# Four instead of two column tiles in the first matmul block, and a last LayerNorm split between VectorE, PSUM and GpSimd, in a decoder layer

## The chip, the cores and the metric

One NeuronCore of a Trainium2 chip runs the whole layer as one launch. The metric is the device time of a run in microseconds. The engines are named as the profile names them: PE is TensorE (PEld its weight loads), DVE is VectorE, ACT is ScalarE, POOL is GpSimd, SP is SyncE, which here only starts transfers.

## The reference

One layer of a hybrid decoder on 512 tokens of width 1024, all in fp32:

```
proj = x @ w_in                          # q, k, v of three token mixers, and gates
m = mixer(...)                           # differential, stick-breaking and dilated attention,
                                         # gated, merged, @ w_out
x = layer_norm(ALPHA * x + m, ln1_g, ln1_b)
c = square(relu(x @ w_up)) @ w_down
ple = sigmoid(x @ w_ple_gate) * (p @ w_ple)
x = layer_norm(ALPHA * x + c + ple, ln2_g, ln2_b)

def layer_norm(x, g, b):
    mu = x.mean(-1); var = square(x - mu).mean(-1)
    return (x - mu) * rsqrt(var + 1e-5) * g + b
```

## The kernel before

Every fp32 operand is split into a rounded high part (`h`, by an ACT cast, line 213) and the remainder (`l`, by a DVE subtraction, line 215), and each product is three matmuls: high by high, high by low, low by high. Weights come in chunks through a ring of SBUF buffers, loaded from SP's queue and split ahead of their use by `pump`. A list `items` holds the matmul groups in their order; the program walks it once and puts between the items the evictions, the splits and the steps of the attention heads. The framework then fixes, for each engine, a static order of instructions and the semaphores between them; an engine works through its own list in order. Dependencies in PSUM are kept for whole tiles (one bank of 512 fp32 columns), not for columns of one.

**The start.** `first_item` (line 293) makes the first two column tiles, T0 (a query tile of the stick-breaking heads) and T1 (a key tile), together: for each of the eight row blocks k of x and w it loads x[k] (256 KB) and w of both tiles (128 KB for one k, 256 KB for a pair of them), splits both, and issues six matmuls of 512 columns. The loads alternate: x0, w0, x1, w1-2, x2, x3, w3-4 and so on. The first `AHEAD` = 4 of them go out at once, the next waits for a matmul of the warm-up on zeros (line 1390). After the block, `t_item` (line 258) makes one further column tile at a time, T2 and T3 first, each from a 512 KB chunk with 24 matmuls (k = 0 to 7); PE then also does the logits of the first head (line 131), which need the split query and key tiles. The low part of the key tile is DVE's line 101 with output `sb_ka`.

**The end.** `plain` (line 1292) makes the last products of the MLP for four row tiles tt = 0 to 3, in halves of 512 columns; for tile three the second half is cut in two groups of 256 columns (`ends`), each in a PSUM bank of its own. Tiles 0 to 2 take their LayerNorm from `layer_norm_act` (line 807): a DVE addition with a row sum, squares on ACT, the power -0.5 on POOL (line 818), centring on DVE (line 820), and a last DVE pass with bias per half, before the store (`rest`, line 822). For tile two that last pass is held back and issued behind the first addition of tile three (`held`, line 1336). Tile three adds its PSUM to the SBUF rows `acc`, takes `bn_stats` per piece (line 1340), and `last_norm` (line 1349) then computes the mean and variance, the inverse root by ACT's square root, a reciprocal and one Newton step on DVE, the centring (line 1359) and the last pass with three stores (lines 1367 and 1369). So that the square root's table is there, line 1981 runs one square root ahead of the last stage.

Of the kernel before, what the change touches and what calls it, by code (L numbers as in the profile page):

```python
# [55 lines left out]
def trunk(tc, a, out):  # L56
    nc = tc.nc
    es = ExitStack()
    with es:
# [73 lines left out]


        RING, RAW = 6, 7
        ORDERED, AHEAD = 17, 4
        loads, chunks, placed = [], [], []
        lows = deque(maxlen=4)
        marks = deque(maxlen=4)
# [153 lines left out]
        def first_item():  # L293

            w = a["w0"].rearrange("p k m -> p (k m)")
            cs = {}
            for k in range(8):
                x_chunk(k)
                if k in (0, 1, 3, 5, 7):
                    n = 256 if k in (0, 7) else 512  # L300
                    c = chunk_of(load(w[:, 256 * k:256 * k + n], n, True))
                    for i in range(n // 256):
                        cs[k + i] = (c, 256 * i)

            def mm(ps):
                for k in range(8):
                    c, o = cs[k]
                    for i, (m, x) in enumerate((("h", xh), ("l", xh), ("h", xl))):
                        for t in range(2):
                            nc.tensor.matmul(ps[t], c[m][:, o + t * P:o + t * P + P], x[k], start=k == 0 and i == 0,  # L310
                                             stop=k == 7 and i == 2, skip_group_check=True)

            def ev(ps):
                for t in range(2):
                    t_evac(*order[t][1:])(ps[t])
            item([cs[k][0] for k in (0, 1, 3, 5, 7)], mm, ev, bank=lambda: (at_bank(), at_bank()))

        HB = slice(0, 256)
        HC = slice(256, 512)
# [484 lines left out]
                                                      ap=[[0, P], [1, 512]]))  # L804
                lnc[n] = t

        def layer_norm_act(ts, sm, g, b, fin):
# [9 lines left out]
            nc.vector.tensor_scalar(r, r, EPS, None, op0=OP.add)  # L817
            nc.gpsimd.tensor_tensor(r, r, mhalf, OP.pow)
            for h in range(2):
                nc.vector.scalar_tensor_tensor(ts[h], ts[h], nmu, lnc[g][h], op0=OP.add, op1=OP.mult)  # L820

            def rest():
                for h in range(2):
                    nc.vector.scalar_tensor_tensor(ts[h], ts[h], r, lnc[b][h], op0=OP.mult, op1=OP.add)
                    fin(h, ts[h])
            return rest

# [463 lines left out]

        def plain(cs, c2, c4, kept):

            sums, held = {}, []
            s6 = slot("bn6e")[:, :18].rearrange("p (a b) -> p a b", b=6)

            ends = [(0, slice(0, 512)), (1, slice(0, 256)), (1, slice(256, 512))]

            def part(tt, half, cc):
                n = cc.stop - cc.start  # L1300
                r = tt % 2
                p, cp = {(0, 0): (2, c2), (1, 0): (4, c4)}.get((tt // 2, half), (0, []))

                def mm(ps):
                    for c, m in zip(cp, (5, 6)):
                        down_mm(ps, m, p, r, c, p == 2 and m == 5, False)
                    for i in range(4):
                        h, lo = left[ND - 1, tt // 2, i % 2]
                        q = slice((i // 2) * 256 + r * P, (i // 2) * 256 + r * P + P)
                        c = cs[i % 2, half]  # L1310
                        s = slice((i // 2) * 512 + cc.start, (i // 2) * 512 + cc.stop)
                        nc.tensor.matmul(ps[:, :n], h[:, q], c["h"][:, s], start=i == 0 and not p, stop=False,
                                         skip_group_check=True)
                        nc.tensor.matmul(ps[:, :n], h[:, q], c["l"][:, s], start=False, stop=False,
                                         skip_group_check=True)
                        nc.tensor.matmul(ps[:, :n], lo[:, q], c["h"][:, s], start=False, stop=i == 3,
                                         skip_group_check=True)

                def ev(ps):
                    t = acc[tt, half]  # L1320
                    if tt < 3:
                        if not half:
                            sums[tt] = small("lsm", 2)
                        nc.vector.scalar_tensor_tensor(t, t, 1.0, ps, op0=OP.mult, op1=OP.add,
                                                       accum_out=sums[tt][:, half:half + 1])
                        if half:
                            def fin(h, y):
                                (nc.sync if h else nc.scalar).dma_start(
                                    out[0, tt * P:tt * P + P, 512 * h:512 * h + 512], y)
                            rest = layer_norm_act([acc[tt, 0], acc[tt, 1]], sums[tt], "ln2_g", "ln2_b", fin)  # L1330
                            if tt == 2:
                                held.append(rest)
                            else:
                                rest()
                        return
                    i = nc.vector.tensor_add(t[:, cc], t[:, cc], ps[:, :n])
# [3 lines left out]
                    nc.vector.bn_stats(s6[:, ends.index((half, cc)), :], t[:, cc])  # L1340
# [5 lines left out]
                item(free, mm, ev, need=list(cs.values()) + list(cp),  # L1346
                     bank=(lambda: kept["y", r]) if p == 4 else at_bank if tt == 3 else None)

            def last_norm():
                ts = [acc[3, 0], acc[3, 1]]  # L1350
                mv = small("mv", 2)
                nc.vector.bn_aggr(mv, s6)

                hv, y, r = [small("lr", 1) for _ in range(3)]
                nc.vector.tensor_scalar(hv, mv[:, 1:2], EPS, -0.5, op0=OP.add, op1=OP.mult)
                nc.scalar.activation(y, hv, AF.Sqrt, scale=-2.0)

                def center(h):
                    nc.vector.scalar_tensor_tensor(ts[h], ts[h], mv[:, 0:1], lnc["ln2_g"][h], op0=OP.subtract,
                                                   op1=OP.mult)  # L1360
                center(0)
                nc.vector.reciprocal(y, y)
                nc.vector.scalar_tensor_tensor(r, y, hv, y, op0=OP.mult, op1=OP.mult)
                nc.vector.scalar_tensor_tensor(r, r, 1.5, y, op0=OP.add, op1=OP.mult)
                center(1)
                for i, (h, cc) in enumerate(ends):
                    nc.vector.scalar_tensor_tensor(ts[h][:, cc], ts[h][:, cc], r, lnc["ln2_b"][h][:, cc],
                                                   op0=OP.mult, op1=OP.add)
                    (nc.scalar if i == 1 else nc.sync).dma_start(
                        out[0, 3 * P:4 * P, 512 * h + cc.start:512 * h + cc.stop], ts[h][:, cc])  # L1370

            for tt in range(3):
                for half in range(2):
# [541 lines left out]
        for n, it in enumerate(items):  # L1915
# [62 lines left out]
                ln_consts("ln1_g", "ln1_b")  # L1978
            if n == ln2_at[0]:

                i = nc.scalar.activation(small("rt", 1), ident[:, 0:1], AF.Sqrt)
                tc.add_manual_dep(getattr(i, "ins", i), lows[-1].name, mybir.DependencyInfo(
                    mybir.DependencyClass.Sync, mybir.DependencyReason.DATA), reason="behind the last gate")
# [54 lines left out]
def _layout(x, p, w_in, da_lambda, da_norm, w_branch_da, w_branch_sb, w_branch_dil, w_out, ln1_g, ln1_b,  # L2038
# [17 lines left out]
    def quarters(w):  # L2056
# [5 lines left out]
        "xn": c(x2.reshape(4, 128, 1024).transpose(1, 0, 2)),  # L2062
        "pT": c(p[0, 0].T.reshape(2, 128, 512).transpose(1, 0, 2)),
        "w0": c(np.stack(tiles[0:2], axis=2).reshape(128, 8, 256)),
        "wt": c(np.stack(tiles[2:])),
        "wv": c(np.stack(vs)),

# [36 lines left out]
```

## Time and profile before

| | us |
|---|---|
| median of three runs (1046.08 to 1046.97) | 1046.86 |
| the profiled execution's own time | 1046.86 |
| its span in the profile | 1044.8 |
| PE busy | 1033.2 |
| DVE busy | 778.0 |
| ACT busy | 588.1 |
| POOL busy | 179.4 |

The span runs from the first to the last record of one execution; the 2.06 us between it and the time lie outside of what the profiler shows. In the views below a row of the timeline is: start, duration, engine, line and operation, output<-inputs, shape, count, and in brackets the engine's idle time ahead of it with what ended it. In a table of windows each engine has its busy time and, in brackets, the number of its instructions.

### The profile page before, as it was taken

The page shows a single profiled execution, that of the slowest core. Times are in us where ns is not written, and L with a number is a line of the kernel's source. Part 1 is how long each engine was busy: PE and PEld are TensorE (multiplying, and loading weights), DVE is VectorE, ACT ScalarE, POOL GpSimd, SP SyncE. Part 2 cuts the span into 40 slices and gives each one's busy share as a digit, 9 for nine tenths or more (in the row PEclk, how much of TensorE's full clock was granted, in tenths as well). Part 3 has the DMA queues.
Part 4 walks back from the last instruction along what each step waited for, and adds up shares of the span by engine and source line. Part 5 has one row for each costly group of instructions (what it writes and reads, how often), then busy time and mean ns, then how long its engine had stood idle before and what let it go on. Part 6 is the DMA issues. An engine that isn't in the chain of part 4 may idle for free.

```text
span 1044.8 us, 15084 instructions
## 1 busy us (share of the span) xinstructions
PE 1033.2 (99%) x5462; PEld 881.3 (84%) x5462; DVE 778.0 (74%) x1392; ACT 588.1 (56%) x1006; POOL 179.4 (17%) x275
## 2 busy tenths in 40 slices
PE   8999999999999999999999999999999999999996
PEld 6887788889888888888888888888999889889885
DVE  6888577768874657789666895798768877877966
ACT  6666445535444545676653753776666556556651
POOL 0013421020212111311211132101221111111000
PEclk9999999999999999999999999999999999999998
DMA  8348999294896996698998998389999999999602
GB/s 321 114 149 269 241 271 267 89 278 141 255 289 170 312 263 157 213 250 278 292 337 275 314 321 261 115 252 302 331 328 345 304 306 281 328 293 338 191 32 81
DMA packets 74346, 260.09 MB, mean 249 GB/s; under 512 B 9144, under 2 KB 10056, under 8 KB 74272
## 3 DMA queue, kind: packets, MB, share of 16 engines
q0 software_dynamic: 33616, 120.40, 44.3%
q1 hardware_dynamic: 40080, 137.81, 36.9%
q8 instruction: 43, 0.70, 0.3%
q10 hardware_dynamic: 576, 0.92, 0.2%
q14 instruction: 31, 0.25, 0.1%
HBM read 256.98 MB, written 111.17 MB: 352 GB/s over the span
## 4 chain that ended last, share of the span: by engine, by line
PE 97%; DVE 1%; DMA 1%; ACT 0%; SPq 0%; issue 0%; DVEq 0%
PE mm L87 11%; PE mm L88 10%; PE mm L89 10%; PE at L1212 4%; PE at L1213 4%; PE at L1214 4%; PE at L558 3%; PE at L560 3%; PE at L559 3%; PE mm L455 2%; PE mm L457 2%; PE mm L456 2%; PE at L89 1%; PE at L87 1%; PE at L88 1%; PE at L849 1%
## 5 line engine op out<-in xcount | busy, mean ns | idle before, releaser
L213 ACT CAST wh<-raw 128x1024 fp32r<-128x1024 f32 x254 | 265.9, 1049 | 241.8 <-PE mm L88 129.1
L215 DVE TENSOR_TENSOR wl<-raw,wh 128x1024 fp32r<-128x1024 f32 x254 | 308.9, 1221 | 119.9 <-ACT wh L213 117.7
L87 PE MATMUL mm<-xhT,wh 128*128 128x512 f32 x304 | 120.8, 397 | 0.0
L89 PE MATMUL mm<-xhT,wl 128*128 128x512 f32 x304 | 119.1, 392 | 0.0
L88 PE MATMUL mm<-xlT,wh 128*128 128x512 f32 x304 | 119.0, 391 | 0.0
L1212 PE MATMUL at<-wh,hh 128*128 128x512 f32 x188 | 73.7, 392 | 0.0
L1213 PE MATMUL at<-wl,hh 128*128 128x512 f32 x188 | 73.7, 392 | 0.0
L87 PE MATMUL mm<-x1hT,wh 128*128 128x256 f32 x256 | 73.6, 288 | 0.0
L1214 PE MATMUL at<-wh,hl 128*128 128x512 f32 x188 | 73.1, 389 | 0.0
L88 PE MATMUL mm<-x1lT,wh 128*128 128x256 f32 x256 | 72.2, 283 | 0.0
L89 PE MATMUL mm<-x1hT,wl 128*128 128x256 f32 x256 | 71.8, 283 | 0.0
L89 PEld LDWEIGHTS mm<-xhT,wl 128*128 128x128 f32 x304 | 57.1, 188 | 12.1
L87 PEld LDWEIGHTS mm<-xhT,wh 128*128 128x128 f32 x304 | 57.2, 188 | 11.6 <-issue 0.4
L88 PEld LDWEIGHTS mm<-xlT,wh 128*128 128x128 f32 x304 | 57.2, 188 | 10.5
L87 PEld LDWEIGHTS mm<-x1hT,wh 128*128 128x128 f32 x256 | 48.8, 190 | 4.6 <-ACT up L1146 2.8
L88 PEld LDWEIGHTS mm<-x1lT,wh 128*128 128x128 f32 x256 | 48.8, 191 | 1.5
L89 PEld LDWEIGHTS mm<-x1hT,wl 128*128 128x128 f32 x256 | 48.6, 191 | 0.0
L1049 POOL DMA_DIRECT2D usum<-in_wu_dram x32 | 27.4, 883 | 86.7 <-DVE wl L215 63.0
L1214 PEld LDWEIGHTS at<-wh,hl 128*128 128x128 f32 x188 | 35.3, 188 | 7.7
L1212 PEld LDWEIGHTS at<-wh,hh 128*128 128x128 f32 x188 | 35.5, 189 | 6.0
L1213 PEld LDWEIGHTS at<-wl,hh 128*128 128x128 f32 x188 | 35.5, 189 | 5.6
L1049 POOL DMA_DIRECT2D dsum<-in_wd_dram x28 | 24.0, 874 | 93.7 <-DVE wl L215 63.0
(606 smaller groups left out, 2673.6 us busy)
## 6 DMA issues: line engine op xcount, KB each, us to landing
usum<-in_wu_dram POOLq DMA_DIRECT2D x48, 512.0 KB, 9.1
dsum<-in_wd_dram POOLq DMA_DIRECT2D x42, 512.0 KB, 9.1
raw<-in_wt_dram SPq DMA_DIRECT2D x38, 512.0 KB, 5.6
msum<-in_wgm_dram POOLq DMA_DIRECT2D x36, 512.0 KB, 9.0
raw<-usum SPq DMA_DIRECT2D x32, 512.0 KB, 7.7
raw<-dsum SPq DMA_DIRECT2D x28, 512.0 KB, 8.1
raw<-in_wd_dram SPq DMA_DIRECT2D x25, 512.0 KB, 5.9
raw<-msum SPq DMA_DIRECT2D x24, 512.0 KB, 7.1
```

Of the source, the lines that this page charges most:

```text
L87: nc.tensor.matmul(ps, wh, xh, start=start, stop=False, skip_group_check=True)
L88: nc.tensor.matmul(ps, wh, xl, start=False, stop=False, skip_group_check=True)
L89: nc.tensor.matmul(ps, wl, xh, start=False, stop=stop, skip_group_check=True)
L213: i = nc.scalar.copy(h, raw)
L215: i = nc.vector.tensor_sub(lo, raw, h.bitcast(F32))
L558: nc.tensor.matmul(ps, h[:, q], c["h"][:, n], start=go, stop=False, skip_group_check=True)
L559: nc.tensor.matmul(ps, h[:, q], c["l"][:, n], start=False, stop=False, skip_group_check=True)
L560: nc.tensor.matmul(ps, lo[:, q], c["h"][:, n], start=False, stop=end, skip_group_check=True)
L1049: i = nc.gpsimd.dma_start(o, i, accum_op=OP.add, max_dma_last_dim=4096)
L1212: nc.tensor.matmul(ps, h[:, q], c["h"][:, s], start=go, stop=False, skip_group_check=True)
L1213: nc.tensor.matmul(ps, h[:, q], c["l"][:, s], start=False, stop=False, skip_group_check=True)
L1214: nc.tensor.matmul(ps, lo[:, q], c["h"][:, s], start=False, stop=end, skip_group_check=True)
```

## The change

Three things are changed together.

1. The first block takes four tiles in its first step. A new input `w1` holds the k = 0 part of the weights of T2 and T3 (128 x 256, 128 KB). It is loaded third, behind x0 and w0, split, and used for six matmuls into the banks of T2 and T3 right behind the first six; `t_item` then starts at k = 1 for these two tiles (21 matmuls instead of 24), though its 512 KB load stays whole. `AHEAD` and the number of ordered loads go up by one.
2. The last passes of tile two leave DVE: ACT multiplies each half by the inverse root, POOL adds the bias, then comes the store.
3. Tile three keeps three of its four quarter pieces in PSUM: the sum is made in place in the bank, `bn_stats` and the centring work there, and the last DVE pass writes to SBUF. The first quarter stays in SBUF, and POOL does its whole last part (centre and scale, gain, bias). The two groups of the second half now lie in one bank. The inverse root is POOL's addition of epsilon and its power -0.5; ACT's square root, the reciprocal, the Newton step and the early square root for the table are gone. There are four stores of 256 columns instead of three.

```diff
-        ORDERED, AHEAD = 17, 4
+        ORDERED, AHEAD = 18, 5
...
+        begun = []
         def t_item(nt, name, j):
...
+            k0 = 1 if nt < 4 else 0
             def mm(ps):
                 c = cs[0]
-                for k in range(8):
+                for k in range(k0, 8):
...
-            item(cs, mm, t_evac(name, j))
+            item(cs, mm, t_evac(name, j), bank=(lambda: begun[nt - 2]) if k0 else None)
...
+                if k == 0:
+                    both = chunk_of(load(a["w1"], 256, True))
+            def step_of(ps, c, o, k):
+                (the six matmuls of one k)
             def mm(ps):
                 for k in range(8):
...
+                    step_of(ps, *cs[k], k)
+                    if k == 0:
+                        begun.extend(mm_bank() for _ in range(2))
+                        step_of(begun, both, 0, 0)
...
             def rest():
                 for h in range(2):
+                    if last:
+                        nc.scalar.activation(ts[h], ts[h], AF.Copy, scale=r)
+                        nc.gpsimd.tensor_tensor(ts[h], ts[h], lnc[b][h], OP.add)
+                    else:
+                        nc.vector.scalar_tensor_tensor(ts[h], ts[h], r, lnc[b][h], op0=OP.mult, op1=OP.add)
                     fin(h, ts[h])
...
-                    i = nc.vector.tensor_add(t[:, cc], t[:, cc], ps[:, :n])
-                    if held:
-                        with tc.issue_after(getattr(i, "ins", i)):
-                            held.pop()()
-                    nc.vector.bn_stats(s6[:, ends.index((half, cc)), :], t[:, cc])
+                    if not half:
+                        nc.vector.tensor_add(t[:, HB], t[:, HB], ps[:, HB])
+                        nc.vector.bn_stats(s6[:, 0, :], t[:, HB])
+                    c = cc if half else HC
+                    nc.vector.tensor_add(ps[:, c], ps[:, c], t[:, c])
+                    nc.vector.bn_stats(s6[:, 1 + ends.index((half, cc)), :], ps[:, c])
...
+                    if half not in held:
+                        held[half] = at_bank()
+                    return held[half]
...
-                (square root on ACT, reciprocal, Newton step, two centrings, three passes, three stores)
+                nc.gpsimd.tensor_scalar(r, mv[:, 1:2], EPS, None, op0=OP.add)
+                nc.gpsimd.tensor_tensor(r, r, mhalf, OP.pow)
...
+                t = ts[0][:, HB]
+                nc.gpsimd.tensor_scalar(t, t, mv[:, 0:1], r, op0=OP.subtract, op1=OP.mult)
+                nc.gpsimd.tensor_tensor(t, t, lnc["ln2_g"][0][:, HB], OP.mult)
+                nc.gpsimd.tensor_tensor(t, t, lnc["ln2_b"][0][:, HB], OP.add)
+                center(1, slice(0, 512))
+                center(0, HC)
+                for i, (h, cc) in enumerate(((1, HB), (1, HC), (0, HC))):
+                    scaled(h, cc)
+                    store(nc.scalar if i == 1 else nc.sync, h, cc)
+                store(nc.scalar, 0, HB)
...
-                i = nc.scalar.activation(small("rt", 1), ident[:, 0:1], AF.Sqrt)
```

In the order of instructions that the framework makes of it, the following differs besides. ACT and DVE evict T0 and T1 one right behind the other, where a weight split stood between them before. The logits of the first head stand behind 17 matmuls of T2; before they stood behind all 24 of T2 and three of T3. The first matmul of tile three's last group waits for a count of DVE's that is reached with the statistics of the group before. On ACT's queue the store of the POOL quarter stands ahead of the store of columns 768 to 1023. Some evictions in the last MLP stage change places by a few instructions.

More of the change, by code (lines that the diff above doesn't have):

```diff
@@ L303, in first_item @@
                         cs[k + i] = (c, 256 * i)
+                if k == 0:
+                    both = chunk_of(load(a["w1"], 256, True))
+            def step_of(ps, c, o, k):
+                for i, (m, x) in enumerate((("h", xh), ("l", xh), ("h", xl))):
+                    for t in range(2):
+                        nc.tensor.matmul(ps[t], c[m][:, o + t * P:o + t * P + P], x[k], start=k == 0 and i == 0,
+                                         stop=k == 7 and i == 2, skip_group_check=True)
             def mm(ps):
                 for k in range(8):
[L307 to L311, printed above, removed]
+                    step_of(ps, *cs[k], k)
+                    if k == 0:
+                        begun.extend(mm_bank() for _ in range(2))
+                        step_of(begun, both, 0, 0)
             def ev(ps):
@@ L315, in ev @@
                     t_evac(*order[t][1:])(ps[t])
-            item([cs[k][0] for k in (0, 1, 3, 5, 7)], mm, ev, bank=lambda: (at_bank(), at_bank()))
+            item([cs[0][0], both] + [cs[k][0] for k in (1, 3, 5, 7)], mm, ev, bank=lambda: (at_bank(), at_bank()))
         HB = slice(0, 256)
@@ L805, in ln_consts, with layer_norm_act @@
                 lnc[n] = t
-        def layer_norm_act(ts, sm, g, b, fin):
+        def layer_norm_act(ts, sm, g, b, fin, last=False):
             sq = small("lsq", 2)
@@ L1292, in plain @@
         def plain(cs, c2, c4, kept):
-            sums, held = {}, []
-            s6 = slot("bn6e")[:, :18].rearrange("p (a b) -> p a b", b=6)
+            sums, held = {}, {}
+            s6 = slot("bn6e")[:, :24].rearrange("p (a b) -> p a b", b=6)
             ends = [(0, slice(0, 512)), (1, slice(0, 256)), (1, slice(256, 512))]
             def part(tt, half, cc):
-                n = cc.stop - cc.start
                 r = tt % 2
@@ L1311, in mm @@
                         s = slice((i // 2) * 512 + cc.start, (i // 2) * 512 + cc.stop)
-                        nc.tensor.matmul(ps[:, :n], h[:, q], c["h"][:, s], start=i == 0 and not p, stop=False,
+                        nc.tensor.matmul(ps[:, cc], h[:, q], c["h"][:, s], start=i == 0 and not p, stop=False,
                                          skip_group_check=True)
-                        nc.tensor.matmul(ps[:, :n], h[:, q], c["l"][:, s], start=False, stop=False,
+                        nc.tensor.matmul(ps[:, cc], h[:, q], c["l"][:, s], start=False, stop=False,
                                          skip_group_check=True)
-                        nc.tensor.matmul(ps[:, :n], lo[:, q], c["h"][:, s], start=False, stop=i == 3,
+                        nc.tensor.matmul(ps[:, cc], lo[:, q], c["h"][:, s], start=False, stop=i == 3,
                                          skip_group_check=True)
@@ L1329, in fin @@
                                     out[0, tt * P:tt * P + P, 512 * h:512 * h + 512], y)
[L1330 to L1334, printed above, removed]
-                        return
-                    i = nc.vector.tensor_add(t[:, cc], t[:, cc], ps[:, :n])
-                    if held:
-                        with tc.issue_after(getattr(i, "ins", i)):
-                            held.pop()()
-                    nc.vector.bn_stats(s6[:, ends.index((half, cc)), :], t[:, cc])
+                            layer_norm_act([acc[tt, 0], acc[tt, 1]], sums[tt], "ln2_g", "ln2_b", fin,
+                                           tt == 2)()
+                        return
+                    if not half:
[4 more added lines that the diff above has]
+                    nc.vector.bn_stats(s6[:, 1 + ends.index((half, cc)), :], ps[:, c])
                     if (half, cc) == ends[2]:
@@ L1345, in part, with bank @@
                     free = list(cs.values())
-                item(free, mm, ev, need=list(cs.values()) + list(cp),
-                     bank=(lambda: kept["y", r]) if p == 4 else at_bank if tt == 3 else None)
+                def bank():
+                    if p == 4:
+                        return kept["y", r]
+                    if tt < 3:
+                        return mm_bank()
+                    if half not in held:
+                        held[half] = at_bank()
+                    return held[half]
@@ L1349, in last_norm @@
+                item(free, mm, ev, need=list(cs.values()) + list(cp), bank=bank)
             def last_norm():
                 ts = [acc[3, 0], acc[3, 1]]
-                mv = small("mv", 2)
+                mv, r = small("mv", 2), small("lr", 1)
                 nc.vector.bn_aggr(mv, s6)
-                hv, y, r = [small("lr", 1) for _ in range(3)]
-                nc.vector.tensor_scalar(hv, mv[:, 1:2], EPS, -0.5, op0=OP.add, op1=OP.mult)
-                nc.scalar.activation(y, hv, AF.Sqrt, scale=-2.0)
@@ L1358, in center @@
[L1358 to L1367, printed above, removed]
-                                                   op0=OP.mult, op1=OP.add)
-                    (nc.scalar if i == 1 else nc.sync).dma_start(
-                        out[0, 3 * P:4 * P, 512 * h + cc.start:512 * h + cc.stop], ts[h][:, cc])
+                nc.gpsimd.tensor_scalar(r, mv[:, 1:2], EPS, None, op0=OP.add)
@@ new lines, in last_norm, with center, scaled @@
+                nc.gpsimd.tensor_tensor(r, r, mhalf, OP.pow)
+                ps = [kept["y", 1], held[1]]
+                def center(h, cc):
+                    nc.vector.scalar_tensor_tensor(ps[h][:, cc], ps[h][:, cc], mv[:, 0:1], lnc["ln2_g"][h][:, cc],
+                                                   op0=OP.subtract, op1=OP.mult)
+                def scaled(h, cc):
+                    nc.vector.scalar_tensor_tensor(ts[h][:, cc], ps[h][:, cc], r, lnc["ln2_b"][h][:, cc],
+                                                   op0=OP.mult, op1=OP.add)
@@ new lines, in store @@
+                def store(q, h, cc):
+                    q.dma_start(out[0, 3 * P:4 * P, 512 * h + cc.start:512 * h + cc.stop], ts[h][:, cc])
+                t = ts[0][:, HB]
[4 more added lines that the diff above has]
+                center(0, HC)
@@ L1979, in trunk @@
             if n == ln2_at[0]:
-                i = nc.scalar.activation(small("rt", 1), ident[:, 0:1], AF.Sqrt)
-                tc.add_manual_dep(getattr(i, "ins", i), lows[-1].name, mybir.DependencyInfo(
-                    mybir.DependencyClass.Sync, mybir.DependencyReason.DATA), reason="behind the last gate")
                 ln_consts("ln2_g", "ln2_b")
@@ L2064, in _layout @@
         "w0": c(np.stack(tiles[0:2], axis=2).reshape(128, 8, 256)),
+        "w1": c(np.stack(tiles[2:4], axis=2).reshape(128, 8, 256)[:, 0]),
         "wt": c(np.stack(tiles[2:])),
```

1 line of the change is left out of this document (removed).

## Prediction

> **What bounds the kernel now.** I read the page's engine shares and its chain first, then a table of windows that cuts the span at the two places the change touches.
>
> ```profile
> PE 1033.2 (99%) x5462; PEld 881.3 (84%) x5462; DVE 778.0 (74%) x1392; ACT 588.1 (56%) x1006; POOL 179.4 (17%) x275
> PE 97%; DVE 1%; DMA 1%; ACT 0%; SPq 0%; issue 0%; DVEq 0%
> 0.00:5.67 5.67, 3.66 (x9) 1.19 (x9) 0.68 (x4) 2.21 (x3) 1.70 (x10) 1.00 0.59 160
> 5.67:18.35 12.68, 12.05 (x49) 9.05 (x50) 10.48 (x19) 8.81 (x14) 0.00 (x0) 1.00 0.99 373
> 18.35:1000.00 981.65, 980.89 (x5234) 840.52 (x5233) 738.06 (x1313) 565.60 (x969) 175.08 (x262) 1.00 0.85 257
> 1033.00:1036.70 3.70, 3.61 (x28) 3.29 (x26) 2.92 (x6) 0.00 (x0) 0.00 (x0) 1.00 0.19 71
> 1036.70:1044.80 8.10, 0.00 (x0) 0.00 (x0) 4.63 (x14) 0.20 (x1) 0.00 (x0) 0.62 0.27 97
> ```
>
> PE is the bound from 5.67 us to the end of its work: between 18.35 and 1000 us it is idle for 0.76 us of 981.65, at a granted clock of 1.00. Neither part of the change removes a matmul, so there are two places to gain: PE's holes inside the first block, and the 8.1 us behind PE's last matmul. What the change reorders in the middle runs under a PE that is busy without a hole, and I cost it at nothing; if that cover were gone it could cost a few tenths, as the 0.76 us of the whole middle shows.
>
> **The start.** PE's timeline, then ACT and DVE in front of it:
>
> ```profile
> 5.67 0.73 PE L310 MATMUL at<-xhT,wh 128*128 128x512 f32 x2 [0.75 <-ACT wh L213]
> ...
> 7.00 0.62 PE L310 MATMUL at<-xlT,wh 128*128 128x512 f32 x2
> 8.22 0.73 PE L310 MATMUL at<-xhT,wh 128*128 128x512 f32 x2 [0.60 <-ACT wh L213]
> 8.95 0.74 PE L310 MATMUL at<-xhT,wl 128*128 128x512 f32 x2
> ...
> 18.19 0.39 PE L87 MATMUL mm<-xhT,wh 128*128 128x512 f32 x1
> 18.41 0.39 PE L88 MATMUL mm<-xlT,wh 128*128 128x512 f32 x1
> ```
>
> ```profile
> 4.70 0.62 ACT L213 CAST xhT<-rawx 128x512 fp32r<-128x512 f32 x1 [2.61 <-DMA rawx<-in_xT_dram]
> ...
> 6.13 0.62 ACT L213 CAST xhT<-rawx 128x512 fp32r<-128x512 f32 x1 [0.51 <-DMA rawx<-in_xT_dram]
> 7.55 0.62 ACT L213 CAST wh<-rawx 128x512 fp32r<-128x512 f32 x1 [0.80 <-DMA rawx<-in_w_dram]
> ...
> 5.96 0.42 DVE L215 TENSOR_TENSOR wl<-rawx,wh 128x256 fp32r<-128x256 f32 x1
> ```
>
> The step k = 0 is over at about 7.46 (7.00 plus two matmuls); k = 1 starts at 8.22, when the weights that landed by 7.55 are cast. One matmul in a run takes 0.227 us (18.19 to 18.41 and on). The change puts six more there: 6 x 0.227 = 1.36 us of work that no longer stands in T2 and T3. Their weights are ready in time: cast behind 5.62, low part behind DVE's 6.38 plus 0.42, so by 6.85. PE is then busy to 7.46 + 1.36 = 8.83.
>
> What it adds in front: 128 KB of load, a cast of 0.40 and a subtraction of 0.42. The loads are in one queue, so x1 and w1-2 land later. Bounds for 128 KB: 0.35 us at the 373 GB/s of the second window, 0.71 as half of what 256 KB took between the casts at 6.13 and 7.55. The cast of w1-2 then ends at 8.5 to 8.9, and k = 1 starts at 8.83 to 8.95. From k = 1 to the first matmul of T2 there are 42 matmuls, 9.55 us in a run; before, it took 18.19 - 8.22 = 9.97, the rest being the wait for the low part at 8.95. I leave 0 to 0.3 of that. T2 resumes at 18.4 to 18.7 instead of 18.19: 0.2 to 0.5 later with 1.36 of work done, a gain of 0.85 to 1.15.
>
> A part is given back at the first head's logits. They need the low part of the key tile:
>
> ```profile
> 21.76 1.23 DVE L215 TENSOR_TENSOR wl<-raw,wh 128x1024 fp32r<-128x1024 f32 x1
> 23.02 0.68 DVE L101 SCALAR_TENSOR_TENSOR sb_ka<-at,sb_ka 64x512 fp32r<-64x512 f32 x1
> ...
> 24.31 0.28 PE L131 MATMUL at<-sb_qa,sb_ka 128*128 128x256 f32 x1
> ```
>
> Before, it ended at 23.70 and PE came at 24.31. In the changed order the 1.23 us split behind which it stood comes later, so it would start at 21.76 and end at 22.44, but PE comes behind only 17 matmuls of T2: 18.19 + 17 x 0.227 = 22.05. Both move by the same 0.2 to 0.5, so PE waits about 0.4 us whatever the loads do. PE's queue is in order: T2's last four matmuls and T3 stand behind. The gain of the start is then 0.45 to 0.75; I take 0.55.
>
> **The end.** PE, then DVE, then the two rows that give the price of one piece, then the stores:
>
> ```profile
> 1034.89 0.28 PE L1316 MATMUL at<-wh,hl 128*128 128x256 f32 x1
> 1035.01 0.28 PE L1312 MATMUL at<-wh,hh 128*128 128x256 f32 x1
> ...
> 1036.33 0.28 PE L1316 MATMUL at<-wh,hl 128*128 128x256 f32 x1
> ```
>
> ```profile
> 1033.78 0.69 DVE L1336 TENSOR_TENSOR xn<-xn,at 128x512 f32<-128x512 f32 x1 [1.82 <-PE at L1316]
> 1034.39 1.41 DVE L824 SCALAR_TENSOR_TENSOR xn<-xn,lr,ln_b 128x512 f32<-128x512 f32 x2
> ...
> 1037.77 0.23 DVE L1352 BATCH_NORM_AGGREGATE mv<-bn6e 128x2 f32<-128x18 f32 x1
> ...
> 1038.11 0.74 DVE L1359 SCALAR_TENSOR_TENSOR xn<-xn,mv,ln_g 128x512 f32<-128x512 f32 x1
> ...
> 1039.93 1.54 DVE L1367 SCALAR_TENSOR_TENSOR xn<-xn,lr,ln_b 128x512 f32<-128x512 f32 x3
> ```
>
> ```profile
> L1336 DVE TENSOR_TENSOR xn<-xn,at 128x256 f32<-128x256 f32 x2 | 0.8, 412 | 0.0
> ...
> L1340 DVE BATCH_NORM_STATS2 bn6e<-xn 128x6 f32<-128x256 f32 x2 | 0.7, 416 | 0.0
> ```
>
> ```profile
> L1369 SPq DMA_DIRECT2D out_dram<-xn x2: 332/332/333, 1040.7 to 1041.5; - x2
> L1369 ACTq DMA_DIRECT2D out_dram<-xn x1: 339/339/339, 1041.1 to 1041.1; - x1
> DMA to landing us min/median/max: 2.1/2.1/2.1
> ```
>
> Gone from DVE's path: the two passes of tile two (1.41), and the three small instructions of the root. Their new homes are idle: ACT from 1032.6 on, POOL as well; even at 2 us each the two POOL additions of tile two end before tile three's root is wanted.
>
> New on PE's path: its last group waits. Before, the groups lay in two banks and PE ran on (1034.89 to 1035.01). In the changed program they share a bank, and the first matmul of the last group waits for DVE's statistics of the group before. DVE does four quarter pieces from 1033.78 to about 1035.35 (adds overlap the statistics ahead of them), then addition 0.41, statistics 0.42, with about 0.02 between: 1036.2. A hand-over takes 0.05 (7.55 + 0.62 to 8.22), so PE restarts at 1036.25 instead of 1035.01: 1.24 us late, and ends at 1036.61 + 1.24, about 1037.9 with the refill. Nothing is queued behind on PE, but DVE's last addition waits for it: addition and statistics to 1038.8, aggregate to 1039.05, one whole centring and one half to 1040.1. Before, the aggregate started at 1037.77 and the last passes at 1039.93.
>
> I weigh one page here. The Trainium skill ("PSUM — Partial Sum Buffer", section on bank collisions) says that two engines must not touch one bank's partitions at once even at different columns, and to guard by bank. By that rule the wait is needed as long as the halves share a bank; by the rows of before alone (no gap between the groups) the end would come out at 0.65 less than before and the whole at 1045.7.
>
> POOL's prices are not in this trace for these forms. The nearest rows:
>
> ```profile
> 0.40 0.12 POOL L2093 MEMSET const-uint8-127<- 128x1 uint8 x1
> ...
> 1.33 0.20 POOL L1402 MEMSET ones_f<- 128x128 f32 x1
> ...
> 1.84 0.31 POOL L1409 MEMSET mask_f<- 128x256 f32 x1
> ...
> 672.61 1.46 POOL L818 TENSOR_TENSOR lr<-lr,mhalf 128x1 f32<-128x1 f32 x1
> 1016.95 1.47 POOL L818 TENSOR_TENSOR lr<-lr,mhalf 128x1 f32<-128x1 f32 x1 [61.50 <-DVE lr L817]
> ...
> 1032.04 0.55 POOL L818 TENSOR_TENSOR lr<-lr,mhalf 128x1 f32<-128x1 f32 x1 [7.41 <-DVE lr L817]
> ```
>
> The addition of epsilon: 0.12 to 0.55, I take 0.3; the power 0.55. The root is there at 1039.05 + 0.05 + 0.3 + 0.05 + 0.55 + 0.05 = 1040.05, level with the centrings. DVE's three quarter passes at 0.40 ((1.54 - 0.74) / 2) end at 1041.3, before it was 1041.47. POOL's three operations on 256 columns: at least 0.31 each (the memset), at most 0.55 plus the 0.21 that the memset grows from 1 to 256 columns, 0.76; I take the middle, 0.55. That ends at 1040.05 + 1.65 + 0.1 = 1041.8. ACT's queue has that store first and the store of another quarter behind it: the second starts at 1041.8 + 0.05 + 0.34 = 1042.2, where the last store of before started at 1041.5. All stores land 2.1 us later, and what follows is the same. The end costs 0.7 us; bounds -0.2 (lowest POOL prices, DVE then sets the end at 1041.3) and +1.6 (highest).
>
> **Sum.** -0.55 + 0.7 = +0.15 us on the profiled execution of 1046.86, which is also the median: 1047.0, in its own bounds 1045.9 to 1048.1. A measurement of this kernel tells about 0.2% (2.1 us) from no change, and this is far inside.
>
> **Rivals.** *Both waits fail to bite.* If the logits wait for nothing and the last group does not stand for DVE, the start gains 1.15; at the end DVE's chain begins at 1036.65 and, with low POOL prices, its last pass ends near 1040.1, 1.4 earlier. Total -2.5: 1044.3. For it: DVE has lost 1.41 us just ahead of the last group. Against it: both waits stand in the program, and 0.83 us of DVE work lies between the groups.
>
> *Slow GpSimd instructions.* The power took 0.55 on most occasions, but 1.46 and 1.47 twice, 0.92 more. Five POOL instructions stand in the last chain, two forms of them new; the first two hold up everything, the other three the ACT stores. One slow one gives 1047.9, three give 0.15 + 2.8: 1049.8, slower. It decides from the second one on (+2.0). Against it: the last two powers of before, close together in time, were both fast.
>
> *The start gives nothing.* If 128 KB delays w1-2 by more than 0.71 and the wait at the logits is 0.8, the block does not do what it is there for: 1047.55. For it: the loads ahead of 7.55 come at well under 373 GB/s (160 in the first window).
>
> **How the numbers follow.** Forecast 0.58, both waits idle 0.16 (0.12 of it past 2.1 us), slow GpSimd 0.13 (0.12 past it; 0.01 more from the forecast's tail), start without gain 0.13. So faster by over 0.2%: 0.12, within 0.75, slower 0.13. The range that leaves out a tenth at each end is 1045.2 to 1048.7.
>
> **What would show it.** Right: the first block's second six matmuls between 7.4 and 8.9 with no hole ahead of k = 1; PE idle about 0.4 us ahead of the first logits at 22 to 23 us, ended by DVE's `sb_ka`; PE idle about 1.2 us between the last two groups, ended by `bn_stats`; the aggregate 1 us later than before against PE's start of the tile; the last store on ACT's queue, behind POOL. Wrong: no hole between the last groups, POOL rows over 0.8 us, or a last store that is SP's.

## The result, and the profile after

The changed kernel takes 1050.41 us (median of six runs; 1050.06 to 1050.55), the kernel before 1046.87 in six runs (1046.08 to 1047.10): a ratio of 1.0035, 95% interval 1.0022 to 1.0048, so 3.5 us slower. The forecast was 1047.0, within 0.2% of no change; its range ended at 1048.7. The profiled execution has a span of 1048.7 us, before 1044.8.

The page first, engine shares and the chain by engine:

```profile
PE 1034.4 (99%) x5462; PEld 881.7 (84%) x5462; DVE 777.0 (74%) x1389; ACT 587.6 (56%) x1006; POOL 185.0 (18%) x282
PE 97%; DVE 1%; ACT 1%; DMA 1%; POOL 0%; issue 0%; SPq 0%; POOLq 0%; ACTq 0%
```

Then the same windows as before, with the last one longer by 3.9:

```profile
5.67:18.35 12.68, 12.05 (x51) 9.38 (x50) 9.41 (x18) 8.63 (x13) 0.00 (x0) 1.00 0.99 365
1033.00:1036.70 3.70, 2.65 (x18) 2.24 (x16) 2.35 (x6) 1.34 (x2) 2.64 (x3) 1.00 0.15 59
1036.70:1048.70 12.00, 1.70 (x12) 1.50 (x12) 3.48 (x9) 0.00 (x0) 3.49 (x5) 0.65 0.20 69
```

PE's work is what it was. It has 1.70 us of matmuls behind 1036.70, where it had none, and POOL, idle there before, is busy for 3.49.

The timeline of the start in the changed kernel: the casts that release PE, the second six matmuls, k = 1, T2 and the first logits.

```profile
7.29 0.62 ACT L213 CAST xhT<-rawx 128x512 fp32r<-128x512 f32 x1 [1.92 <-DMA rawx<-in_xT_dram]
8.45 0.62 ACT L213 CAST wh<-rawx 128x512 fp32r<-128x512 f32 x1 [0.54 <-DMA rawx<-in_w_dram]
...
7.88 0.61 PE L313 MATMUL mm<-xlT,wh 128*128 128x512 f32 x2
9.12 0.73 PE L313 MATMUL at<-xhT,wh 128*128 128x512 f32 x2 [0.63 <-ACT wh L213]
9.85 0.74 PE L313 MATMUL at<-xhT,wl 128*128 128x512 f32 x2
...
19.09 0.39 PE L87 MATMUL mm<-xhT,wh 128*128 128x512 f32 x1
...
23.39 0.39 PE L131 MATMUL at<-sb_qa,sb_ka 128*128 128x256 f32 x1 [0.29 <-DVE sb_ka L101]
```

In this execution the hole ahead of k = 1 is still there, 0.63 (before 0.60), only later, because x1 and w1-2 are cast 1.16 and 0.90 us later. T2 begins 0.90 later than before with 1.36 us of work done ahead of it; the logits then wait for `sb_ka`. The hole is no fixed part of the new start: in the profiles of e1 and e4 below, which have the same start, it is not there.

The timeline of the end, PE, DVE and POOL in turn, then the stores:

```profile
1034.05 0.28 PE L1325 MATMUL at<-wh,hh 128*128 128x256 f32 x1
...
1035.37 0.28 PE L1329 MATMUL at<-wh,hl 128*128 128x256 f32 x1
1036.79 0.39 PE L1325 MATMUL at<-wh,hh 128*128 128x256 f32 x1 [1.14 <-DVE bn6e L1352]
...
1038.52 0.43 DVE L1351 TENSOR_TENSOR at<-at,xn 128x256 f32<-128x256 f32 x1 [1.79 <-PE at L1329]
...
1039.46 0.26 DVE L1371 BATCH_NORM_AGGREGATE mv<-bn6e 128x2 f32<-128x24 f32 x1
1040.82 1.26 DVE L1381 SCALAR_TENSOR_TENSOR xn<-at,lr,ln_b 128x256 f32<-128x256 f32 x3
...
1033.95 2.52 POOL L836 TENSOR_TENSOR xn<-xn,ln_b 128x512 f32<-128x512 f32 x2 [0.84 <-ACT xn L835]
1039.82 0.24 POOL L1372 TENSOR_SCALAR lr<-mv 128x1 f32<-128x1 f32 x1 [3.34 <-DVE mv L1371]
1040.14 0.57 POOL L1373 TENSOR_TENSOR lr<-lr,mhalf 128x1 f32<-128x1 f32 x1
1040.82 1.24 POOL L1387 TENSOR_SCALAR xn<-xn,mv,lr 128x256 f32<-128x256 f32 x1
1042.14 0.72 POOL L1388 TENSOR_TENSOR xn<-xn,ln_g 128x256 f32<-128x256 f32 x1
1042.94 0.72 POOL L1389 TENSOR_TENSOR xn<-xn,ln_b 128x256 f32<-128x256 f32 x1
...
1043.70 0.82 ACTq L1385 DMA_DIRECT2D out_dram<-xn  x2
```

DVE is through at 1042.08, POOL at 1043.66. And then there is a part that the prediction did not look at, the instructions with which the program closes on each engine. In the view of one source line, before and then after (count, shortest/median/longest in ns, first and last start in us):

```profile
L2100 POOLq DRAIN  x3: 46/102/4432, 1032.0 to 1044.5; - x3
L2100 SPq DRAIN  x3: 7/7/7, 1044.0 to 1044.3; - x3
...
L2100 DVEq DRAIN  x2: 19/798/1578, 1040.0 to 1044.3; - x2
```

```profile
L2123 POOLq DRAIN  x3: 102/193/4608, 1042.9 to 1048.3; - x3
L2123 SPq DRAIN  x3: 7/7/7, 1046.3 to 1047.8; - x3
```

GpSimd's first closing DRAIN, the longest of its three, starts while its last instruction still runs. Before, the last was the power of tile two, 1032.04 + 0.55 = 1032.59; the DRAIN ran from 1032.0 for 4.43 us to 1036.4, 3.8 behind it, beside other work. SP's own DRAIN came at 1044.0, when the last store had landed, and the program closed 0.8 later. DVE's DRAIN is long too, 1.58, but it ends about 0.1 behind DVE's last pass (1041.47); only GpSimd's runs on for long behind its engine's work. After, POOL's last addition ends at 1043.66, and the DRAIN runs from 1042.9 for 4.61 us to 1047.5: again 3.9 behind it. SP is through at 1046.3, so for 1.2 us nothing is left to do but this DRAIN. The 3.9 us by which the span grew are then 2.3 of stores that land later (1046.3 against 1044.0), 1.2 of the DRAIN behind them, and 0.4 in the last exchange, which took 1.2 instead of 0.8.

### The profile page after: what moved, and what is told of

Its sections match the earlier page's. It is cut to its first block, busy times and chain, and to the rows that moved or that the text cites. A ratio compares the mean times of both kernels' runs of the same rounds, so it can differ in the third digit from the quotient of the medians.

```text
span 1048.7 us, 15103 instructions
## 1 busy us (share of the span) xinstructions
PE 1034.4 (99%) x5462; PEld 881.7 (84%) x5462; DVE 777.0 (74%) x1389; ACT 587.6 (56%) x1006; POOL 185.0 (18%) x282
## 4 chain that ended last, share of the span: by engine, by line
PE 97%; DVE 1%; ACT 1%; DMA 1%; POOL 0%; issue 0%; SPq 0%; POOLq 0%; ACTq 0%
PE mm L87 10%; PE mm L89 10%; PE mm L88 10%; PE at L1226 4%; PE at L1227 4%; PE at L1228 4%; PE at L568 3%; PE at L570 3%; PE at L569 3%; PE mm L465 2%; PE mm L467 2%; PE mm L466 2%; PE at L89 1%; PE at L87 1%; PE at L88 1%; PE at L863 1%
```

## The experiments

Theory A: the loss lies in the tail and has two causes, the wait for the shared bank and a closing DRAIN on GpSimd that ends 3.9 us behind its last instruction, whatever that is; the start gives nothing. Rival B: the reordered start is the main cost. Rival C: POOL's quarter is slow and its store late, but nothing else hangs on POOL. The runs were made in three groups on three chips (e1 to e4, e5 to e8, e9 to e11). "Before" in the ratios is the kernel before on the chip of the group, 1046.45, 1046.61 and 1046.78 us, each over 21 to 33 runs. The changed kernel itself was not run again in these groups, so a difference to its 1050.41 carries an uncertainty of some 0.4 us, by which the kernel before differs between them.

**e1 and e2: start and tail apart.** The two halves of the change, cut to what tells them:

```diff
+            k0 = 1 if nt < 4 else 0                                   # e1: all up to first_item
+                    both = chunk_of(load(a["w1"], 256, True))
...
+                nc.gpsimd.tensor_tensor(r, r, mhalf, OP.pow)          # e2: all in layer_norm_act and plain
```

> The changed start (first block of four tiles, one more load of x ahead of w1's second part) with the tail of before. Theory A (the end is set by GpSimd's closing work, some 3.9 us behind its last instruction, and the start gives nothing): this start reaches equal matmul counts at the same time as before and only the order of the last evictions adds 0 to 0.5 us, so 1046.9 to 1047.4. Rival B (the reordered start and what it moves behind it is the main cost): 1048.5 or more.

> The start of before with the changed tail. Theory A: all of the loss but the 0.47 us with which TensorE entered the tail late, so about 1050.0. Rival B (start is the main cost): under 1049.

Measured: e1 1046.83 (ratio 1.0005, 0.9996 to 1.0014), e2 1049.97 (1.0034, 1.0021 to 1.0047). The tail alone has the whole loss, 3.5; B falls.

**e5 and e6: one more small POOL instruction, late or early,** in the kernel before:

```diff
                         out[0, 3 * P:4 * P, 512 * h + cc.start:512 * h + cc.stop], ts[h][:, cc])
+                nc.gpsimd.tensor_tensor(small("lr", 1), ts[1][:, 511:512], mhalf, OP.mult)   # e5
+                nc.gpsimd.tensor_tensor(small("lr", 1), mv[:, 0:1], mhalf, OP.mult)          # e6
```

> The kernel before, plus one GpSimd multiplication of 128x1 elements that waits for VectorE's last pass; its result is not used and the output is the same. Theory A: that instruction ends near 1041.7 us, GpSimd's closing work some 3.9 behind it near 1045.6, and with 1.2 for the closing exchange the span ends near 1046.8 instead of 1044.8: about 1048.6, 1.9 slower than before. Rival C (no closing work behind GpSimd's last instruction): the last store still sets the end, 0 to 0.1 slower.

> The kernel before, plus the same GpSimd multiplication, but waiting only for the aggregate of the last tile's statistics (near 1037.8 us); its result is not used and the output is the same. Theory A: the closing work ends near 1042.3, before the last store has landed, so no change to before (within 0.2). Rival (one more GpSimd instruction at the end costs in itself, wherever it stands): as much as the late one.

Measured: e5 1048.12 (1.0015, 1.0006 to 1.0023), e6 1046.52 (1.0001, 0.9992 to 1.0010). e5's late instruction in its timeline and its closing line, then the same of e6:

```profile
1041.97 0.19 POOL L1371 TENSOR_TENSOR lr<-xn,mhalf 128x1 f32<-128x1 f32 x1 [8.97 <-DVE xn L1367]
```

```profile
L2101 POOLq DRAIN  x3: 46/93/4071, 1041.9 to 1046.5; - x3
L2101 SPq DRAIN  x3: 7/7/7, 1044.4 to 1046.3; - x3
```

```profile
1038.75 0.19 POOL L1371 TENSOR_TENSOR lr<-mv,mhalf 128x1 f32<-128x1 f32 x1 [5.50 <-DVE mv L1352]
```

```profile
L2101 POOLq DRAIN  x3: 46/93/4072, 1038.7 to 1045.2; - x3
L2101 SPq DRAIN  x3: 7/7/7, 1044.6 to 1044.9; - x3
```

An instruction of 0.19 us whose result nobody reads costs 1.5 us where it is POOL's last at 1042.16 (its DRAIN ends at 1046.0, 1.6 behind SP), and nothing at 1038.94 (1042.8, ahead of SP). C falls, for something else does hang on POOL: this is the instruction's place, not its length. I expected 1.9, because I took the closing exchange behind the DRAIN from the changed kernel (1048.7 - 1047.5 = 1.2); in e5 it takes 0.8 (1046.8 - 1046.0), as before.

**e10: one more POOL instruction of 1.2 us, with VectorE idle:**

```diff
+                g = lnc["ln2_g"][0][:, HB]
+                nc.gpsimd.tensor_scalar(g, g, mv[:, 0:1], r, op0=OP.subtract, op1=OP.mult)
```

> The changed kernel, with one more GpSimd tensor_scalar of 128x256 (the same form as the first of its three, on a constant that nothing reads any more) behind GpSimd's last addition, when VectorE is idle; the output is the same. If the price of 1.24 us is the instruction's own: again 1.24, and by theory A (GpSimd's closing work 3.86 behind its last instruction) the end moves by 1.3, to 1051.7. If the 1.24 came from VectorE running beside it: 0.7 to 0.8, and the end moves by 0.8, to 1051.2. If the end does not hang on GpSimd's last instruction: 1050.4.

Measured: 1051.32 (1.0043, 1.0031 to 1.0056). POOL's timeline and its closing line:

```profile
1040.51 1.24 POOL L1387 TENSOR_SCALAR xn<-xn,mv,lr 128x256 f32<-128x256 f32 x1
...
1043.35 1.22 POOL L1391 TENSOR_SCALAR ln_g<-ln_g,mv,lr 128x256 f32<-128x256 f32 x1
```

```profile
L2125 POOLq DRAIN  x3: 46/93/5809, 1042.6 to 1049.2; - x3
```

The price is the instruction's own: 1.22 with DVE idle, 1.24 beside DVE's passes. The DRAIN grew by 1.20 (5.81 against 4.61) and ended at 1048.4, again 3.9 behind POOL's end at 1044.57. The time alone, 0.9 above the changed kernel, would have pointed at the contention rival; but this execution reached its tail 0.31 earlier (POOL's first piece 1040.51 against 1040.82), which the rows show and the time does not.

**e4: the quarter back on VectorE.** POOL keeps only the root; the quarter is centred and scaled by two more DVE passes ahead of its store.

```diff
-                nc.gpsimd.tensor_scalar(t, t, mv[:, 0:1], r, op0=OP.subtract, op1=OP.mult)
-                nc.gpsimd.tensor_tensor(t, t, lnc["ln2_g"][0][:, HB], OP.mult)
-                nc.gpsimd.tensor_tensor(t, t, lnc["ln2_b"][0][:, HB], OP.add)
...
+                nc.vector.scalar_tensor_tensor(t, t, mv[:, 0:1], lnc["ln2_g"][0][:, HB], op0=OP.subtract,
+                                               op1=OP.mult)
...
+                nc.vector.scalar_tensor_tensor(t, t, r, lnc["ln2_b"][0][:, HB], op0=OP.mult, op1=OP.add)
```

> The changed kernel, but the last quarter of the rows is normalized by VectorE like the other three; GpSimd keeps only the inverse root. Theory A: GpSimd's last instruction then ends near 1040.7 us instead of 1043.66, its closing work ends near 1044.6, and VectorE's last pass (near 1042.9) with its store sets the end: about 1047.6. Rival C (no closing work; the order of ScalarE's two stores and the late quarter alone set the end): the store of the last quarter starts 0.8 us earlier and lands 0.8 earlier, about 1049.6.

Measured: 1047.42 (1.0009, 1.0000 to 1.0017), 3.0 below the changed kernel. Its POOL and its closing line:

```profile
1039.20 0.57 POOL L1373 TENSOR_TENSOR lr<-lr,mhalf 128x1 f32<-128x1 f32 x1
```

```profile
L2123 POOLq DRAIN  x3: 46/93/4454, 1039.2 to 1044.5; - x3
L2123 SPq DRAIN  x3: 7/7/7, 1044.0 to 1044.3; - x3
```

The DRAIN ends at 1043.7, ahead of SP's 1044.0: hidden again, and C's 1049.6 is not what came. Against its own before e4 is 1.0 slower, against the changed kernel's 3.5: by that reckoning 2.6 are returned. From DVE's first addition of tile three (1033.33, in the changed kernel 1034.25) to the end the two profiles differ by 3.0.

**e3: banks of their own for the last two groups.**

```diff
-                    if half not in held:
-                        held[half] = at_bank()
-                    return held[half]
+                    held[half, cc.start] = at_bank()
+                    return held[half, cc.start]
```

> The changed kernel, but TensorE's last two groups write PSUM banks of their own, so that the last group need not wait for the statistics of the one before. Theory A: the whole tail moves up by the 1.3 us of that wait, to about 1049.1. If the wait is covered by VectorE's queue of adds and statistics: 1050.4, unchanged.

Measured: 1048.93 (1.0023, 1.0014 to 1.0033), 1.5 below the changed kernel; by the ratios to their own befores, 1.1. PE's last groups and the statistics behind:

```profile
1035.23 0.28 PE L1325 MATMUL at<-wh,hh 128*128 128x256 f32 x1
...
1036.87 0.43 DVE L1351 TENSOR_TENSOR at<-at,xn 128x256 f32<-128x256 f32 x1 [0.39 <-PE at L1329]
```

PE runs on without a hole, and DVE's last addition starts 1.65 earlier (1036.87 against 1038.52), 0.25 of it because PE came to the tail that much earlier here.

**e7: the extra load from another queue.** The start of e1, with

```diff
-                        i = nc.sync.dma_start(s["raw"], s["src"])
+                        i = (nc.scalar if s.get("act") else nc.sync).dma_start(s["raw"], s["src"])
...
+                    both["from"]["act"] = True
```

> The changed start with the tail of before, and the load of w1's first part issued from ScalarE's queue instead of SP's, so that one issue less (0.42 to 0.47 us) stands ahead of each later load on SP. If the time of issue is what delayed x1 and w1's second part in the changed start: k = 1 begins 0.4 to 0.5 earlier than with the same start without this edit, and the time falls by 0.3 to 0.5. If the bandwidth of the loads is what delayed them: the same as that start, within 0.2.

Measured: 1046.08 (0.9994, 0.9985 to 1.0003), 0.75 below e1, which ran on another chip; against their own befores the two are 0.9 apart. SP's issues, the casts and k = 1 in e7, then SP's issues in the changed kernel:

```profile
1.25 0.42 SPq L181 DMA_DIRECT2D rawx<-in_w_dram  x1
1.72 0.42 SPq L181 DMA_DIRECT2D rawx<-in_xT_dram  x1
2.19 0.43 SPq L181 DMA_DIRECT2D rawx<-in_w_dram  x1
...
5.52 0.62 ACT L213 CAST xhT<-rawx 128x512 fp32r<-128x512 f32 x1
6.93 0.62 ACT L213 CAST wh<-rawx 128x512 fp32r<-128x512 f32 x1 [0.79 <-DMA rawx<-in_w_dram]
...
8.93 0.61 PE L314 MATMUL at<-xhT,wh 128*128 128x512 f32 x2
9.38 0.62 PE L314 MATMUL at<-xhT,wl 128*128 128x512 f32 x2
```

```profile
1.24 0.89 SPq L181 DMA_DIRECT2D rawx<-in_w_dram  x2
2.17 0.43 SPq L181 DMA_DIRECT2D rawx<-in_xT_dram  x1
2.65 0.43 SPq L181 DMA_DIRECT2D rawx<-in_w_dram  x1
```

Each load on SP costs 0.42 of issue and 0.05 between two; with the extra one elsewhere, x1 goes out at 1.72 instead of 2.17. The landings scatter more than that from profile to profile, so here are all profiles, grouped by their start: x1's cast, k = 1, T2's first matmul, and PE's 251st matmul, by which all have done the same work.

| start | profiles | x1 cast | k = 1 | T2 | 251st, mean |
|---|---|---|---|---|---|
| before | 5 | 5.88 to 7.66 | 7.49 to 9.00 | 17.82 to 18.95 | 59.24 |
| changed, load on SP | 6 | 6.39 to 7.85 | 8.42 to 9.22 | 18.34 to 19.16 | 59.10 |
| changed, load on ACT | 2 | 5.52, 5.66 | 8.93, 8.72 | 18.45, 18.25 | 58.55 |

On SP the start gains 0.14 on the mean, inside a scatter of 1.1; on ACT's queue 0.69, but these are two profiles (58.45 and 58.66), and one of the six on SP (e4, 58.56) lies between them. I had expected k = 1 to come earlier on ACT's queue. It does not, but it runs on: the 42 matmuls to T2 take 9.52 there, 9.92 to 9.97 on SP. The rows show why. On SP the second pair of k = 1, which needs the low part of the weights, starts 0.72 or 0.73 behind the first in all six profiles; on ACT's queue it is 0.45, because that low part is ready at 8.27 in e7, ahead of k = 1. x1 is cast 1.7 earlier there on the mean, more than the 0.45 of its issue; where the rest comes from is open.

**e8, e9 and e11: what can be had.** e8 is the start of before with a tail that leaves POOL nothing behind the root: tile two's last pass on ACT and POOL as changed, tile three's sums in PSUM in banks of their own, all passes on DVE and three stores. Against the changed tail:

```diff
-                nc.gpsimd.tensor_scalar(t, t, mv[:, 0:1], r, op0=OP.subtract, op1=OP.mult)
-                (gain and bias on POOL, passes and four stores)
+                for h, cc in ends:
+                    center(h, cc)
+                for i, (h, cc) in enumerate(ends):
+                    scaled(h, cc)
+                    store(nc.scalar if i == 1 else nc.sync, h, cc)
```

e9 joins it to e7's start, e11 to the start as changed.

> The start of before, and of the changed tail only what does not put GpSimd last: tile two's rest shared between ScalarE and GpSimd, tile three's sums in PSUM banks of their own, the inverse root by GpSimd's power, all passes and the statistics on VectorE. Theory A: the aggregate is ready as in before or somewhat earlier, GpSimd's last instruction ends near 1038.8 and its closing work near 1042.7, hidden behind the last store; VectorE's last pass ends near 1040.5 against 1041.5: about 1045.7, 0.8 to 1.0 faster than before. Rival (sums in PSUM cost VectorE as much as they save): no change.

> The changed start with its extra load issued from ScalarE's queue, and the tail that keeps GpSimd off the end. If the two gains are independent, their sum against before: -0.6 from that start and -0.4 from that tail, so about 1045.6. If the start's gain was only a lucky landing of its loads: -0.4, as with that tail alone.

> As the kernel with both (changed start, tail that keeps GpSimd off the end), but the extra load issued from SP's queue as in the change. If the issue on SP is what made the loads late and ate the start's gain: 0.4 to 0.8 slower than its twin, about 1046.2. If the queue makes no difference: the same as its twin within 0.2.

Measured: e8 1046.16 (0.9996, 0.9987 to 1.0005), e9 1045.67 (0.9994, 0.9985 to 1.0003), e11 1046.45 (0.9996, 0.9987 to 1.0005). e9 is 4.7 below the changed kernel. Against the kernel before it is 1.1 lower by medians, but its interval holds 1, as do e7's and e8's: a gain of that size is not shown. e8's 0.45 is half of the 0.8 to 1.0 that I expected. The queue of the one load made 0.75 and 0.78 by medians in its two pairs of twins (e1 and e7, e11 and e9), the same way both times. But e9 is split, eight runs at 1045.0 to 1046.1 and three at 1047.3 to 1047.4, above all of e11's; the means are only 0.4 apart. That the queue is worth 0.8 is likely, not shown.

## Why the prediction was wrong, point by point

**The step that failed:** "All stores land 2.1 us later, and what follows is the same." What follows is SP's collecting of the stores or GpSimd's DRAIN, whichever is later. Even with my own end of POOL, 1041.8, a DRAIN 3.9 behind it ends at 1045.7; with the exchange of 0.8 that is 1046.5, 1.7 over the span of before, where I had +0.7. e5 shows this cost by itself. It stood in the trace of before as a 4.43 us record on POOL's queue, hidden by 7.6 us. The end was missed by 3.2 us of span (+3.9 against +0.7): 1.0 is this step with POOL ending where I had it, 1.9 is POOL ending later than I had it (1043.66 against 1041.8), and 0.4 is the longer exchange.

**The term that was mis-sized:** POOL's three operations, "I take the middle, 0.55" within 0.31 to 0.76. They took 1.24, 0.72 and 0.72, with 0.08 between: 2.84 from first to last, where I had 1.75. That is 1.1 of the 1.9; the other 0.8 is their later start, 1040.82 against 1040.05, from the aggregate below. It also makes the stores late, so without any DRAIN the end would still have been 2.3 later than before by the rows. The first lay outside of its bounds, because a memset, which reads nothing, does not bound an instruction that reads a tile and two scalars per row. For the two `tensor_tensor` operations, gain and bias, the Trainium skill ("GPSIMD Engine Reference", section on performance versus the Vector engine) gives about 2.6 cycles per element at 1.2 GHz; that is an estimate of 0.55 us for 256 columns before its dispatch, and the rows (0.72 for 256 columns, 1.26 each for the 512 of tile two) grow by 0.54 for 256 columns, so they agree. The Trainium skill's remark on the same page, in the section on engine selection, that one-input operations run at about line rate (by its 1.2 GHz an estimate of 0.2 us here) does not hold for `tensor_scalar` with two scalars per row: 1.24.

**The shared bank: right.** 1.24 expected, and PE's restart came 1.30 late (1035.37 + 0.12 to 1036.79), ended by `bn6e` as said; e3 puts its worth at 1.1 to 1.5 us of the total, and 1.4 by the rows (1.65 less 0.25). The aggregate ended at 1039.72 (1039.46 + 0.26) where I had 1039.05: 0.67 late, of which 0.47 is PE's later entry into the tail (its first 256-column matmul at 1034.05, before at 1033.58). Profiles of one program differ by as much there: e5 and e6, which are the kernel before up to that point, have DVE's first addition of tile three at 1034.20 and 1034.45, before 1033.78. So I do not assign it to the change. No run here lets TensorE and VectorE into one bank at the same time, so what that would do is not shown.

**The root: nearly right.** The addition of epsilon took 0.24 (0.3), the power 0.57 (0.55).

**The start: its mechanism right, its gain not.** I gave 0.35 to 0.71 for the delay by the 128 KB, from bandwidth alone; SP's 0.47 for issuing it was left out, though the diff puts the load into that queue ahead of x1. On the mean of the profiles x1 is cast 0.9 later than with the start of before, which holds both. k = 1 at "8.83 to 8.95" fits the mean of the six SP profiles, 8.93, which scatter from 8.42 to 9.22, so that is in part luck. Of the 0.42 that PE loses on the way to T2, which I put at 0 to 0.3, 0.40 remained: the wait for the low part of the weights is still there. With the load on ACT's queue it went. The wait at the logits is 0.29 in all eight profiles of this start, whatever the loads did, as the prediction argued; I had 0.4.

**The rivals.** "Both waits fail to bite" is ruled out by the rows. "Slow GpSimd instructions" gave 1049.8 and comes near in size, but by another mechanism: the forms' own price, the same in all four profiles that have them (after, e2, e3, e10), not single instructions at 0.92 more. "The start gives nothing" is what happened within the scatter, but the 0.55 that it would take from the sum is a small part of the miss. The upper end of my sum's own bounds is 1048.0 by its terms (1046.86 - 0.45 + 1.6), not 1048.1.

**The sum, from e2 and its parts:** the tail costs 3.5 us. Against the changed kernel, own banks return 1.1 to 1.5 (e3), the quarter on DVE 2.6 to 3.0 (e4), and both together 3.9 to 4.0 (e11); the lower figures are those against each group's own before. The new last passes of tile two, on ACT and POOL, were not tried alone; e8 and e11 keep them and are no slower than before.

## What to carry to other kernels

Ask of every engine when its last instruction ends, and what closes behind it. The view of the last source line has the closing records; what counts is where an engine's longest one ends, not its length, because it can begin while the last instruction still runs. Its end less the end of that instruction, 3.9 us for GpSimd here, says how far ahead of the last landed store the engine must be finished to cost nothing. A helper engine at the end of a kernel should get work that ends first, not last. And a load that is put ahead of others costs the queue's time to issue it (0.47 us here) as well as its bytes; another engine's idle queue may take it, though what that is worth lies inside the intervals here.

## What the runs showed of the hardware

- GpSimd's closing DRAIN ends 3.8 to 3.9 us behind its last compute instruction in all thirteen profiles, whether that was 0.19 or 1.22 us long. What it does in this time no run shows.
- The exchange behind the last of SP's and GpSimd's DRAINs took 0.8 us before, in e4 and in e5, 1.2 in the changed kernel, e2 and e3 and 1.1 in e10, which all have POOL's quarter; why is open.
- A 128x256 `tensor_scalar` with two scalars per row takes 1.22 to 1.24 us on GpSimd; a `scalar_tensor_tensor` pass of DVE over as many columns took 0.47 in the changed kernel (three in 1.26, overlapped).
- A load's landing in the first 8 us scatters by over 1 us between profiles with the same start (x1's cast 5.88 to 7.66 in the five with the start of before), more than the edit there could give.
